# Down weights of a ConvFFN: loads apart from their parts and begun within the up stage, sums on VectorE, another order of products, the last pair loaded twice

## The chip, the cores and the metric

The kernel runs on one core of one Trainium2 chip. The metric is the device time of one launch in microseconds, the median of several runs. One execution was also recorded by the hardware profiler; all rows below are from that one. In rows, PE is TensorE's matmuls, PEld its weight loads, DVE is VectorE, ACT ScalarE, POOL GpSimd and SP (SPq for its DMA issues) SyncE. "L1226" is line 1226 of the kernel before.

## The reference

One step of a hybrid network over 2048 latent tokens (on a grid 64 wide) and 128 context tokens, width 1024: an HGRN2 mixer, then a ConvFFN, then a final norm. The part that matters here is the ConvFFN, with 2816 inner channels:

```
def conv_ffn(h, w_up, conv_w, conv_b, w_down, grid_axis):
    a, g = jnp.split(h @ w_up, 2, axis=-1)
    a = token_conv(a, conv_w, conv_b, grid_axis)
    return (jax.nn.silu(a) * g) @ w_down
```

`token_conv` adds, for each channel, the neighbours left and right with weights of their own. The result is added to the stream under a gate, and `rms_norm` follows.

## The kernel before

Every float32 product is made of three float16 products: an operand is split into a high part (ScalarE, `A.activation` with `Copy`) and the rest (VectorE), and high x high, high x low and low x high are summed in PSUM. In rows such parts of the down weights are `wd`: L1226 makes the high part on ScalarE, L1227 the low part on VectorE, both from `rawd`, the float32 block loaded from memory.

Both matrix products of the ConvFFN over latent tokens use a Strassen-Winograd scheme: blocks of 2 x 2, seven products instead of eight. `PROD` names for each product the weight block or sum (A11 to A22, S1 to S4), the token block or sum (B11, T1, ...) and the PSUM bank (A, B or C) that it accumulates in. The context tokens use the plain three products (`mm3`).

The **up stage** goes over pairs of channel blocks (`cb` = 0, 2, ... 20) and in each over four pieces `p` of 512 latent tokens; after p = 1 the context follows (`up_ctx`). A pass `up(cb, p)` has seven products for two column blocks, 14 x 12 matmuls of 256 columns. Between products, `post()` runs one step of each of the generators that wait in `gates` and `pending`: `gate` does the convolution (L1103 on ScalarE, L1110 and L1112 on VectorE), silu (L1137), the multiplication by g (L1139), and the sums and splits of the tokens that the down stage needs (L1147 to L1151, L970, L971), and stores them in memory (`ud`, `uc` for the context). `c` are the products' results in SBUF: L1085 to L1097 put them there from PSUM on ScalarE, L1082 adds to them on VectorE.

The **down stage** holds all weights in SBUF: four pairs `i` of output blocks, for each four blocks A11 to A22 (`blocks_down`) and four sums S1 to S4 (`sums_down`), each 128 x 1408. The token side is read from memory again (`load_ut`, tiles `U`), one product ahead. First come the context (`down_ctx`) and product 1 of the first piece, pair by pair, then all other products of the four pieces in the order of `todo`; each adds its result to `x` at once (L1303, for the context L1270), and after the last that touches a half the final norm runs (`final_norm`, L360 to L368).

Each engine works through its own list in order. The lists are written by a scheduler that may move an instruction of the program ahead of others on the same engine, and the places of SBUF tiles are found by `place()` from the tiles' lifetimes in program order: a tile waits until the last reader of what lay there before is done. All loads and stores go through SyncE's one queue.

Of the kernel before, what the change touches and what calls it, by code (L numbers as in the profile page):

```python
# [23 lines left out]
NCTX = 128  # L24
NTOK = NLAT + NCTX
NCB = 22
# [82 lines left out]
def place(tiles, far):  # L109
# [6 lines left out]
    for grain, lo, hi, some in (  # L116
# [5 lines left out]
        some.sort(key=lambda i: (age(i) < NEVER // 2, size(i) != 11, age(i) <= AGE,  # L122
                                 -min(size(i), 16), tiles[i].born))
        tight = []
        while True:
            lives = [[] for _ in range(slots)]
            bad = None
            for i in some:
# [5 lines left out]
                if n == 11:  # L134
                    cap = 1
# [79 lines left out]
def stages(nc, tl, pt, drt, xT, adaH, adaT, pvec, w_in, w_out, w_up, w_down, state, yT, st_out):  # L215
# [944 lines left out]
    def up(cb, p):  # L1160
# [5 lines left out]
        for i in (1, 2, 6, 5, 7, 3, 4):  # L1166
            while any(PROD[i][0] not in WQ.get((cb, j), {}) for j in range(2)):
                post()
            for j in range(2):
                product(qs[j], i, WQ[cb, j], TT[p])  # L1170
            post()
            tick()
        gates.append(gate(cb, p, *qs))
# [55 lines left out]
    def blocks_down(i):  # L1229
        load_rd(i)  # L1230
# [4 lines left out]
        a11, a12, a21, a22 = (RD[i][z] for z in ("A11", "A12", "A21", "A22"))  # L1235
        G.tensor_tensor(a22, a21, a22, ALU.add)
        G.tensor_tensor(a21, a11, a21, ALU.subtract)
        G.tensor_tensor(a11, a22, a11, ALU.subtract)
        G.tensor_tensor(a12, a12, a11, ALU.subtract)

    def sums_down(i):
        for z, b in (("S2", "A11"), ("S1", "A22"), ("S3", "A21"), ("S4", "A12")):
            part(i, z, RD[i][b])
            yield

# [123 lines left out]
    for cb in range(0, NCB, 2):  # L1369
        last = cb + 2 == NCB  # L1370
        for p in range(CTX):
# [5 lines left out]
            if last and p < 2:  # L1377
                pending.append(blocks_down(p))
            if last and p == 2:
                while pending:  # L1380
                    post()
                load_uc()
                for j in range(2):
                    load_xd(CTX, j, 0, NCTX)
    while gates:
        post()
    load_ut(0, PROD[1][1])
    load_xd(0, 0, 0)
    pending.extend([blocks_down(2), blocks_down(3), *(sums_down(i) for i in range(MP))])
    for i in range(MP):  # L1390
        while "A22" not in DW[i]:
            post()
        down_ctx(i)
        tick()
        post()
        if i % 2:
            down(0, 1, (i - 1, i))
    final_norm(CTX, 0, NCTX)
    NEED = {1: (0, 0), 6: (0, 1), 5: (1, 1), 4: (1, 0)}
    todo = [(p, n) for p in range(CTX)  # L1400
            for n in ((1, 2, 6, 5, 7, 3, 4), (1, 6, 5, 7, 3, 2, 4))[p == CTX - 1]]
    for k, (p, n) in enumerate(todo):
        if k + 1 < len(todo):
# [4 lines left out]
        if k + 1 < len(todo) and n1 in NEED:  # L1408
# [5 lines left out]

# [46 lines left out]
```

## Time and profile before

| what | value |
| --- | --- |
| median of three runs | 2813.37 us (2812.61 to 2813.89) |
| profiled execution | 2808.24 us |
| span in its profile | 2806.1 us |
| mean granted clock of TensorE | 0.990 |
| busy TensorE / VectorE / ScalarE / GpSimd | 2707.9 / 1896.1 / 1068.8 / 131.8 us |

The profiled execution's time is its span and some 2 us around it. Busy times are sums over an engine's instructions; matmuls that run at the half clock count with their longer time. The up stage lies between about 1395 and 2307 us, the down stage behind it.

### The profile page before, as it was taken

To read this page: it belongs to the slowest core of one execution; us is meant where nothing else is said; L and a number is where in the kernel's file an instruction comes from. 1 tells how busy PE (TensorE), PEld (TensorE's weight loads), DVE (VectorE), ACT (ScalarE), POOL (GpSimd) and SP (SyncE) were. 2 spreads that over 40 slices of the span, in tenths; PEclk is the share of its full clock that TensorE was granted. 3 is DMA by queue.
4 is the path that set the end of the run, shared out by engine and by line. 5 is a ranking of instruction groups with operands and counts; after the bars stand their busy time and mean duration, and the time that the engine had idled before them with its cause. 6 is when DMAs were issued, how large, how long until landed. Compare 5 with 4: busy or idle time off the path is not lost.

```text
span 2806.1 us, 57255 instructions
## 1 busy us (share of the span) xinstructions
PE 2707.9 (97%) x23576; PEld 2129.9 (76%) x23576; DVE 1896.1 (68%) x5308; ACT 1068.8 (38%) x2373; POOL 131.8 (5%) x100
## 2 busy tenths in 40 slices
PE   8999999999999999999999999999999976999998
PEld 4677777777777776754588888888888866888887
DVE  7987788878876677746996767676666777233133
ACT  5533333333334342424664545454445433000001
POOL 0100000000000000000000000000000124000000
PEclk9999999999999999999999999999999998999999
DMA  7021212121101010434122222222221353343342
GB/s 269 20 63 40 78 34 77 43 70 45 66 9 51 9 52 16 148 111 179 61 59 82 60 77 80 70 73 74 84 86 57 101 170 110 106 153 133 125 147 88
DMA packets 188309, 236.85 MB, mean 84 GB/s; under 512 B 12304, under 2 KB 142736, under 8 KB 188048
## 3 DMA queue, kind: packets, MB, share of 16 engines
q1 hardware_dynamic: 188048, 233.19, 26.3%
q8 instruction: 185, 3.03, 0.4%
q14 instruction: 76, 0.62, 0.1%
HBM read 163.55 MB, written 69.60 MB: 83 GB/s over the span
## 4 chain that ended last, share of the span: by engine, by line
PE 72%; DVE 15%; DMA 5%; ACT 3%; issue 2%; POOL 0%; SPq 0%; DVEq 0%; POOLq 0%; ACTq 0%
PE pj_p L1076 11%; PE pj_p L1294 10%; PE sc_p L1076 8%; PE pj_p L417 7%; PE pj_p L418 7%; PE pj_p L416 7%; PE pj_p L540 4%; PE pj_p L538 4%; PE pj_p L539 4%; PE sc_p L692 2%; PE sc_p L1294 2%; DMA ud<-u 2%; DMA r<-w_up 1%; PE sc_p L652 1%; PE sc_p L661 1%
## 5 line engine op out<-in xcount | busy, mean ns | idle before, releaser
L1076 PEld LDWEIGHTS <-w 128*128 128x128 f16 x7392 | 725.3, 98 | 126.0 <-issue 40.0
L1076 PE MATMUL pj_p<-T,w 128*128 128x256 f16 x4224 | 491.4, 274 | 33.8 <-DVE c L1082 10.4
L1294 PEld LDWEIGHTS <-wd 128*128 128x128 f16 x3696 | 364.7, 99 | 80.7 <-issue 19.7
L1294 PE MATMUL pj_p<-U,wd 128*128 128x256 f16 x3168 | 358.5, 274 | 21.4 <-DVE x L1303 11.7
L1076 PE MATMUL sc_p<-T,w 128*128 128x256 f16 x3168 | 369.2, 273 | 1.6 <-ACT c L1091 1.6
L416 PE MATMUL pj_p<-H,wp 128*128 128x512 f16 x768 | 290.6, 379 | 3.7 <-ACT H L395 3.4
L417 PE MATMUL pj_p<-H,wp 128*128 128x512 f16 x768 | 291.7, 380 | 0.9 <-DVE H L400 0.9
L418 PE MATMUL pj_p<-H,wp 128*128 128x512 f16 x768 | 291.6, 380 | 0.0
L540 PE MATMUL pj_p<-wp,H 128*128 128x256 f16 x1024 | 279.2, 273 | 0.0
L539 PE MATMUL pj_p<-wp,H 128*128 128x256 f16 x1024 | 279.1, 273 | 0.0
L538 PE MATMUL pj_p<-wp,H 128*128 128x256 f16 x1024 | 279.1, 273 | 0.0
L1303 DVE SCALAR_TENSOR_TENSOR x<-pj_p,g,x 128x256 f32<-128x256 f32 x96 | 46.3, 483 | 231.9 <-PE pj_p L1294 227.5
L418 PEld LDWEIGHTS <-wp 128*128 128x128 f16 x960 | 94.0, 98 | 91.4 <-issue 2.2
L416 PEld LDWEIGHTS <-wp 128*128 128x128 f16 x960 | 94.2, 98 | 83.9 <-issue 4.4
L417 PEld LDWEIGHTS <-wp 128*128 128x128 f16 x960 | 94.0, 98 | 80.8 <-issue 1.4
L1103 ACT ACTIVATE y<-c,pv,cws 128x512 f32<-128x512 f32 x88 | 71.4, 813 | 153.2 <-DVE c L1082 147.1
L363 ACT ACTIVATE n<-x 128x256 f32<-128x256 f32 (+1 forms) x63 | 23.4, 398 | 277.2 <-DVE x L1303 225.2
L511 ACT ACTIVATE f<-pj_p 128x512 f32<-128x512 f32 x64 | 38.1, 597 | 196.4 <-PE pj_p L418 196.4
L540 PEld LDWEIGHTS <-H 128*128 128x128 f16 x1024 | 100.2, 98 | 11.9
L539 PEld LDWEIGHTS <-H 128*128 128x128 f16 x1024 | 100.2, 98 | 11.8
L538 PEld LDWEIGHTS <-H 128*128 128x128 f16 x1024 | 100.3, 98 | 11.5
L417 PE MATMUL pj_p<-og,wo 128*128 128x512 f16 (+1 forms) x320 | 108.7, 349 | 0.0
(281 smaller groups left out, 5095.3 us busy)
## 6 DMA issues: line engine op xcount, KB each, us to landing
ud<-u SPq DMA_DIRECT2D x44, 896.0 KB, 4.8
U<-ud SPq DMA_DIRECT2D x56, 704.0 KB, 4.5
r<-w_up SPq DMA_DIRECT2D x44, 512.0 KB, 3.7
wr<-w_in SPq DMA_DIRECT2D x40, 512.0 KB, 4.2
wr<-adaT SPq DMA_DIRECT2D x32, 512.0 KB, 3.6
rawd<-w_down SPq DMA_DIRECT2D x16, 704.0 KB, 6.3
x<-xT SPq DMA_DIRECT2D x32, 256.0 KB, 5.4
sp<-oT SPq DMA_DIRECT2D x32, 256.0 KB, 2.5
```

The source lines that it names most:

```text
L416: T.matmul(out, whl[0], hhl[:, 0, :n], start=first, stop=False)
L417: T.matmul(out, whl[0], hhl[:, 1, :n], start=False, stop=False)
L418: T.matmul(out, whl[1], hhl[:, 0, :n], start=False, stop=last)
L511: A.activation(ft, pj[:, :n], AF.Tanh, scale=0.5 * IWS)
L538: T.matmul(o, hp[k][:, 0, tok], wvg[0][:, k], start=(k == 0), stop=False)
L539: T.matmul(o, hp[k][:, 0, tok], wvg[1][:, k], start=False, stop=False)
L540: T.matmul(o, hp[k][:, 1, tok], wvg[0][:, k], start=False, stop=(k == KT - 1))
L692: T.matmul(pkv[:, d, cc_], un["kT"][:, d, cc_], vt[:, cc_], start=True, stop=True)
L1076: T.matmul(out, wt[:, a, ks], tt[:, b, k], start=first and k == 0 and n == 0, stop=i in (2, 3, 4) and k == 3 and n == 2, skip_group_check= ...
L1103: A.activation(y, a, AF.Identity, bias=pv[:, PV_CB + cb : PV_CB + cb + 1], scale=cws[:, 22 + cb : 23 + cb])
L1294: T.matmul(out, w[:, a, k], UT[p, zb][b][:, k], start=first and i % 2 == 0 and k == 0 and q == 0, stop=n in (2, 3, 4) and k == KP - 1 and ...
L1303: V.scalar_tensor_tensor(x, get(src), g64[:, 1, m, 0:1], x, ALU.mult, ALU.add)
```

## The change

What it does: the raw loads of the down weights (`load_rd`) stand apart from the making of their parts, and the loads for pairs 0 to 2 are issued while the last pair of channel blocks is still in the up stage. There too, behind product 6 of the last pass, the context's tokens (`load_uc`), the first `U` and the `x` of context and first piece are loaded. The sums S1 to S4 are made by VectorE instead of GpSimd, and the parts S2 and S3 are made for each pair right behind its sums, S1 and S4 of all pairs afterwards. Product 1 of the first two pairs comes before the context of pair 2, and the context of pair 3 behind product 1 of all pairs. The four raw blocks of pair 3 are loaded a second time for the sums. All four pieces use the order 1, 2, 6, 7, 4, 5, 3, and `place()` treats tiles of 22 grains as those of 11 (a grain is 512 bytes of a partition; `rawd`, `wd` and `U` have 11).

```
--- before.py
+++ after.py
@@ -119,7 +119,7 @@
         slots = (hi - lo) // grain
         size = lambda i: -(-tiles[i].size // grain)
         age = lambda i: tiles[i].last - tiles[i].born
-        some.sort(key=lambda i: (age(i) < NEVER // 2, size(i) != 11, age(i) <= AGE,
+        some.sort(key=lambda i: (age(i) < NEVER // 2, size(i) not in (11, 22), size(i) != 11, age(i) <= AGE,
                                  -min(size(i), 16), tiles[i].born))
         tight = []
         while True:
@@ -131,7 +131,7 @@
                 for a, b in tight:
                     if t.born <= b and a <= t.last:
                         cap >>= 1
-                if n == 11:
+                if n in (11, 22):
                     cap = 1
                 cap = max(cap, 1)
                 room = []
@@ -1170,6 +1170,12 @@
                 product(qs[j], i, WQ[cb, j], TT[p])
             post()
             tick()
+            if i == 6 and cb + 2 == NCB and p + 1 == CTX:
+                load_uc()
+                load_ut(0, "B11")
+                for j in range(2):
+                    load_xd(CTX, j, 0, NCTX)
+                load_xd(0, 0, 0)
         gates.append(gate(cb, p, *qs))
 
     def gate_ctx(cb, a, g):
@@ -1227,21 +1233,28 @@
         V.scalar_tensor_tensor(t[:, 1], src, WS, t[:, 0], ALU.mult, ALU.subtract)
 
     def blocks_down(i):
-        load_rd(i)
         for z in ("A11", "A12", "A21", "A22"):
             part(i, z, RD[i][z])
             yield
 
-        a11, a12, a21, a22 = (RD[i][z] for z in ("A11", "A12", "A21", "A22"))
-        G.tensor_tensor(a22, a21, a22, ALU.add)
-        G.tensor_tensor(a21, a11, a21, ALU.subtract)
-        G.tensor_tensor(a11, a22, a11, ALU.subtract)
-        G.tensor_tensor(a12, a12, a11, ALU.subtract)
-
-    def sums_down(i):
-        for z, b in (("S2", "A11"), ("S1", "A22"), ("S3", "A21"), ("S4", "A12")):
-            part(i, z, RD[i][b])
+    def sums_down(pairs):
+
+        for i in pairs:
+            a11, a12, a21, a22 = (RD[i][z] for z in ("A11", "A12", "A21", "A22"))
+            V.tensor_tensor(a22, a21, a22, ALU.add)
+            V.tensor_tensor(a21, a11, a21, ALU.subtract)
             yield
+            V.tensor_tensor(a11, a22, a11, ALU.subtract)
+            V.tensor_tensor(a12, a12, a11, ALU.subtract)
+            yield
+            part(i, "S2", a11)
+            yield
+            part(i, "S3", a21)
+            yield
+        for i in pairs:
+            for z, b in (("S1", "A22"), ("S4", "A12")):
+                part(i, z, RD[i][b])
+                yield
 
     def load_xd(p, j, h, n=HN):
 
@@ -1374,44 +1387,46 @@
                 up_ctx(cb)
                 if not last:
                     pending.extend([quad(cb + 2, 0), quad(cb + 2, 1)])
-            if last and p < 2:
-                pending.append(blocks_down(p))
-            if last and p == 2:
-                while pending:
-                    post()
-                load_uc()
-                for j in range(2):
-                    load_xd(CTX, j, 0, NCTX)
-    while gates:
-        post()
-    load_ut(0, PROD[1][1])
-    load_xd(0, 0, 0)
-    pending.extend([blocks_down(2), blocks_down(3), *(sums_down(i) for i in range(MP))])
-    for i in range(MP):
-        while "A22" not in DW[i]:
-            post()
+            if last and p == 0:
+                load_rd(0)
+            if last and p == 1:
+                load_rd(1)
+                load_rd(2)
+                pending.extend([blocks_down(0), blocks_down(1)])
+    load_rd(3)
+    load_ut(0, "B21")
+    for i in range(2):
         down_ctx(i)
         tick()
         post()
-        if i % 2:
-            down(0, 1, (i - 1, i))
+    pending.append(blocks_down(2))
+    down(0, 1, (0, 1))
+    while "A22" not in DW[2]:
+        post()
+    down_ctx(2)
+    pending.append(blocks_down(3))
+    down(0, 1, (2, 3))
+    while "A22" not in DW[3]:
+        post()
+    down_ctx(3)
     final_norm(CTX, 0, NCTX)
-    NEED = {1: (0, 0), 6: (0, 1), 5: (1, 1), 4: (1, 0)}
-    todo = [(p, n) for p in range(CTX)
-            for n in ((1, 2, 6, 5, 7, 3, 4), (1, 6, 5, 7, 3, 2, 4))[p == CTX - 1]]
+    load_rd(3)
+    pending.append(sums_down(range(MP)))
+    tick()
+    NEED = {1: (0, 0), 6: (0, 1), 7: (1, 1), 4: (1, 0)}
+    todo = [(p, n) for p in range(CTX) for n in (1, 2, 6, 7, 4, 5, 3)]
     for k, (p, n) in enumerate(todo):
-        if k + 1 < len(todo):
+        if k + 1 < len(todo) and k:
             p1, n1 = todo[k + 1]
             load_ut(p1, PROD[n1][1])
         if k:
             down(p, n)
-        if k + 1 < len(todo) and n1 in NEED:
+        if k and k + 1 < len(todo) and n1 in NEED:
             load_xd(p1, *NEED[n1])
         if n in (3, 4):
             final_norm(p, int(n == 3), HN)
     while norms:
         tick()
-
 
 # ---- launch: one core; inputs laid out by the host, outputs as the reference has them ----
```

The lists of instructions, as the scheduler orders them. GpSimd's list in the down stage, difference of the two kernels, its first sums (`rawd` are the raw blocks, the sums overwrite them):

```order
-L1236 TENSOR_TENSOR rawd_28490<-rawd_28488,rawd_28490 128x1408
-L1237 TENSOR_TENSOR rawd_28488<-rawd_28484,rawd_28488 128x1408
-L1238 TENSOR_TENSOR rawd_28484<-rawd_28490,rawd_28484 128x1408
-L1239 TENSOR_TENSOR rawd_28486<-rawd_28486,rawd_28484 128x1408
-L1236 TENSOR_TENSOR rawd_28928<-rawd_28926,rawd_28928 128x1408
```

All 16 are gone from this list. VectorE's list around the start of the down stage, from the last gate's multiplication (L1139) to the first read of product 1's result into `x`, before (`wd` is a low part, `y` the gate's tile; conv and context rows left out):

```order
L1139 TENSOR_TENSOR y_29286<-y_29286,c_2960_29072 128x1024
...
L1227 SCALAR_TENSOR_TENSOR wd_29659<-rawd_29651,wd_29659 128x1408
...
L1227 SCALAR_TENSOR_TENSOR wd_29606<-rawd_29460,wd_29606 128x1408
L1227 SCALAR_TENSOR_TENSOR wd_29464<-rawd_29456,wd_29464 128x1408
L1227 SCALAR_TENSOR_TENSOR wd_29848<-rawd_28490,wd_29848 128x1408
...
L1227 SCALAR_TENSOR_TENSOR wd_29662<-rawd_29653,wd_29662 128x1408
...
L1227 SCALAR_TENSOR_TENSOR wd_29609<-rawd_29462,wd_29609 128x1408
L1303 SCALAR_TENSOR_TENSOR x_29315<-pj_p_29612,g_2050_15449,x_29315 128x256
```

and now:

```order
L1139 TENSOR_TENSOR y_29443<-y_29443,c_2960_29058 128x1024
...
L1233 SCALAR_TENSOR_TENSOR wd_29666<-rawd_28810,wd_29666 128x1408
...
L1233 SCALAR_TENSOR_TENSOR wd_29851<-rawd_29295,wd_29851 128x1408
L1233 SCALAR_TENSOR_TENSOR wd_29622<-rawd_28804,wd_29622 128x1408
L1233 SCALAR_TENSOR_TENSOR wd_29854<-rawd_29297,wd_29854 128x1408
...
L1244 TENSOR_TENSOR rawd_28810<-rawd_28808,rawd_28810 128x1408
L1233 SCALAR_TENSOR_TENSOR wd_29896<-rawd_29301,wd_29896 128x1408
...
L1245 TENSOR_TENSOR rawd_28808<-rawd_28804,rawd_28808 128x1408
L1233 SCALAR_TENSOR_TENSOR wd_29625<-rawd_28806,wd_29625 128x1408
L1247 TENSOR_TENSOR rawd_28804<-rawd_28810,rawd_28804 128x1408
L1316 SCALAR_TENSOR_TENSOR x_29167<-pj_p_29586,g_2050_15449,x_29167 128x256
```

Between the same two rows stand now two more kinds of row, the sums L1244, L1245 and L1247, among the parts (now L1233); parts for the pairs 2 and 3 are mixed. SyncE's list in the last block of the up stage, before (`ud` and `uc` are stores of u, the others are loads):

```order
L1251 DMA x_29061<-xsp_17507 128x128 x4
L1222 DMA rawd_28488<-w_down 128x11x128
L1222 DMA rawd_28490<-w_down 128x11x128
L1158 DMA ud_15452<-u_28622 1792x1x256
L1222 DMA rawd_28924<-w_down 128x11x128
L1185 DMA uc<-u_28811 128x256
L1222 DMA rawd_28926<-w_down 128x11x128
L1185 DMA uc<-u_28881 128x256
L1222 DMA rawd_28922<-w_down 128x11x128
L1222 DMA rawd_28928<-w_down 128x11x128
L1158 DMA ud_15453<-u_28908 1792x1x256
```

and now:

```order
L1228 DMA rawd_28800<-w_down 128x11x128
L1158 DMA ud_15452<-u_28606 1792x1x256
L1228 DMA rawd_28804<-w_down 128x11x128
L1228 DMA rawd_28806<-w_down 128x11x128
L1228 DMA rawd_28798<-w_down 128x11x128
L1228 DMA rawd_28796<-w_down 128x11x128
L1228 DMA rawd_28808<-w_down 128x11x128
L1228 DMA rawd_28810<-w_down 128x11x128
L1191 DMA uc<-u_28795 128x256
L1158 DMA ud_15453<-u_28908 1792x1x256
L1191 DMA uc<-u_28881 128x256
L1270 DMA U_29149<-uc 128x2816
```

Raw loads that stood one or two at a time between the stores now stand ahead of them, and those of `U` follow right behind the stores.

## Rows read from the trace of the kernel before

**Rows 1.** The page, its part on busy time: busy us of each engine, share of the span and number of instructions.

```profile
PE 2707.9 (97%) x23576; PEld 2129.9 (76%) x23576; DVE 1896.1 (68%) x5308; ACT 1068.8 (38%) x2373; POOL 131.8 (5%) x100
```

**Rows 2.** Busy time by stretches around the end of the up stage: stretch, its length, then for PE, PEld, DVE, ACT and POOL busy us and instructions, last PE's granted clock, the DMA share and GB/s.

```profile
2204.00:2250.00 46.00, 42.99 (x435) 38.38 (x434) 34.34 (x41) 20.09 (x36) 12.45 (x4) 1.00 0.40 110
2250.00:2300.00 50.00, 33.55 (x273) 28.25 (x273) 38.84 (x48) 21.05 (x42) 14.31 (x5) 0.88 0.52 154
...
2350.00:2400.00 50.00, 28.59 (x190) 21.73 (x189) 29.10 (x25) 14.17 (x17) 12.72 (x4) 0.76 0.19 60
```

**Rows 3.** The waits of TensorE between 2204 and 2430 us, longest sums first: line, what it waited for, us in total, times, longest.

```profile
PE pj_p L1076 <- ACT c L1089: 8.8, 1, 8.8
PE pj_p L1294 <- DVE x L1303: 8.5, 4, 4.9
PE sc_p L1294 <- DMA U<-ud: 7.3, 1, 7.3
PE pj_p L1076 <- ACT y L1199: 5.4, 1, 5.4
PE pj_p L1294 <- DMA U<-ud: 4.8, 2, 3.9
PE pj_p L1294 <- ACT wd L1226: 3.7, 1, 3.7
```

**Rows 4.** Groups of TensorE's instructions between 2204 and 2430 us, by form: line, names, shapes, count, busy us and mean ns of one, idle time before them. L1294 are the down products, L1076 the up products; L416 is the first of the three lines of `mm3`, each with the same count.

```profile
L1294 PE MATMUL pj_p<-U,wd 128*128 128x256 f16 x400 | 49.7, 288 | 18.2 <-DVE x L1303 8.5 <-DMA U<-ud 4.8 <-ACT wd L1226 3.7
L1076 PE MATMUL pj_p<-T,w 128*128 128x256 f16 x387 | 47.7, 282 | 18.0 <-ACT c L1089 8.8 <-ACT y L1199 5.4 <-ACT y L1198 2.3
L1076 PE MATMUL sc_p<-T,w 128*128 128x256 f16 x288 | 34.8, 279 | 1.4 <-ACT c L1091 1.4
...
L416 PE MATMUL pj_p<-U,wd 128*128 128x128 f16 x176 | 29.6, 219 | 0.0
...
L1294 PE MATMUL sc_p<-U,wd 128*128 128x256 f16 x132 | 17.9, 303 | 7.7 <-DMA U<-ud 7.3 <-DVE x L1303 0.5
L416 PE MATMUL pj_p<-T,w 128*128 128x128 f16 x32 | 5.4, 219 | 0.0
```

**Rows 5.** The course of TensorE: start, us, instruction, count in a row, idle time before it and who ended it. The first row is the first matmul of the down stage; the second and third are the first and last of 77 matmuls of 128 columns that lie in between, one row each.

```profile
2307.51 0.22 PE L416 MATMUL pj_p<-U,wd 128*128 128x128 f16 x1
...
2339.80 0.22 PE L416 MATMUL pj_p<-U,wd 128*128 128x128 f16 x1
...
2344.04 0.22 PE L417 MATMUL pj_p<-U,wd 128*128 128x128 f16 x1
...
2387.46 6.63 PE L1294 MATMUL sc_p<-U,wd 128*128 128x256 f16 x33 [7.29 <-DMA U<-ud]
...
2403.70 3.77 PE L1294 MATMUL sc_p<-U,wd 128*128 128x256 f16 x33
2407.30 5.51 PE L1294 MATMUL pj_p<-U,wd 128*128 128x256 f16 x49
```

**Rows 6.** The course of GpSimd between 2230 and 2370 us: the first and the last of its 16 sums, which are all that it does there.

```profile
2237.32 3.22 POOL L1236 TENSOR_TENSOR rawd<-rawd,rawd 128x1408 f32<-128x1408 f32 x1 [832.95 <-PE pj_p L1076]
...
2357.91 4.42 POOL L1239 TENSOR_TENSOR rawd<-rawd,rawd 128x1408 f32<-128x1408 f32 x1
```

**Rows 7.** The course of VectorE: two rows from beside GpSimd's first sums, and one from between them and the next four, when GpSimd does nothing.

```profile
2237.55 3.27 DVE L1151 TENSOR_TENSOR t<-y,t 128x256 f32<-128x256 f32 x1
2240.74 0.74 DVE L1082 SCALAR_TENSOR_TENSOR c<-pj_p,c 128x256 f32<-128x256 f32 x2
...
2267.17 0.41 DVE L1151 TENSOR_TENSOR t<-y,t 128x256 f32<-128x256 f32 x1
```

**Rows 8.** The chain that ended last, two pieces of it: start, us on the chain, what.

```profile
2280.09 6.64 DVE y L1110 x2
...
2290.21 3.63 DVE y L1112
...
2298.22 1.87 PE pj_p L1076 x8
...
2381.49 5.93 DMA U<-ud
```

**Rows 9.** Groups of VectorE's instructions between 2204 and 2430 us, by form, columns as in rows 4.

```profile
L1227 DVE SCALAR_TENSOR_TENSOR wd<-rawd,wd 128x1408 f16<-128x1408 f32 x32 | 66.9, 2103 | 29.0 <-ACT wd L1226 29.0
...
L1139 DVE TENSOR_TENSOR y<-y,c 128x1024 f32<-128x1024 f32 x5 | 6.1, 1225 | 4.7 <-ACT y L1137 4.7
```

**Rows 10.** The course of VectorE behind the end of the up stage, with GpSimd idle: the last conv from its first to its last row, and two low parts in a row.

```profile
2308.46 1.39 DVE L1110 SCALAR_TENSOR_TENSOR y<-c,cws,y 128x504 f32<-128x504 f32 x2
...
2315.22 0.42 DVE L1151 TENSOR_TENSOR t<-y,t 128x256 f32<-128x256 f32 x1
...
2322.08 3.16 DVE L1227 SCALAR_TENSOR_TENSOR wd<-rawd,wd 128x1408 f16<-128x1408 f32 x2 [0.30 <-ACT wd L1226]
```

**Rows 11.** The course of ScalarE: two high parts of down weights that wait for their raw blocks.

```profile
2274.04 1.38 ACT L1226 ACTIVATE wd<-rawd 128x1408 f16<-128x1408 f32 x1 [2.13 <-DMA rawd<-w_down]
2276.30 1.38 ACT L1226 ACTIVATE wd<-rawd 128x1408 f16<-128x1408 f32 x1 [0.88 <-DMA rawd<-w_down]
```

**Rows 12.** The waits of TensorE in the whole execution, columns as in rows 3: up products for VectorE's adds, and norms.

```profile
PE pj_p L1076 <- DVE c L1082: 10.4, 12, 2.5
...
PE sc_p L368 <- DVE n L364: 5.2, 6, 1.6
```

## Prediction, made before the changed kernel ran

> **What bounds the kernel now.** I read the page first, then the busy time by stretches, the waits of TensorE, and last the engines beside it. The page's first line [rows 1] has TensorE busy in 97% of the span, so time can only come from the 3% or from matmuls that run slowly while they count as busy. The table by stretches [rows 2] shows where both lie: between 2250 and 2300 us TensorE is busy 33.55 of 50 us at a granted clock of 0.88, between 2350 and 2400 us 28.59 of 50 at 0.76. That is the passage from the up stage to the down stage, which is what the change rewrites.
>
> How much is lost there: between 2204 and 2430 us (226 us) TensorE runs 400 + 387 + 288 + 132 = 1207 matmuls of 256 columns, and 3 x (176 + 32) = 624 of 128 columns [rows 4]. Undisturbed, 33 of the first kind go by in 3.60 us (2403.70 to 2407.30), 0.109 each, and 77 of the second kind in 4.24 us, 0.055 each [rows 5]. So the work is 1207 x 0.109 + 624 x 0.0556 = 131.8 + 34.7 = 166.5 us, and **59.5 us are lost**. The waits of that window say to whom: six rows add up to 38.5 us [rows 3]. The other 21 us are smaller waits and half clock: after one wait 33 matmuls take 6.63 us, later 3.77 [rows 5]. Some 24.6 us of the loss fall before the up stage ends at 2307.51 [rows 5], since 672 + 96 matmuls, 73.4 + 5.3 us, fill the 103.3 us from 2204.2 on.
>
> The waits have one root more than their names tell. GpSimd runs 16 sums of the down weights, the first at 2237 us in 3.2 us, the last at 2358 in 4.4 [rows 6]. Beside one of them VectorE's L1151 takes 3.27 us; without one the same operation takes 0.41. L1082, which reads one operand from PSUM, stays short beside them (two in 0.74) [rows 7]. The chain that ended last shows the price [rows 8]: two conv operations L1110 take 6.64 us, L1112 another 3.63 in the chain, the gate comes late, and TensorE's next matmul stands at 2298.22, after the longest wait of the window, 8.8 us. In the second half the weights' low parts (L1227) and the loads are late: the load of U that TensorE waits for 7.3 us is issued only at 2381.49 and takes 5.93 [rows 8].
>
> The Trainium skill (SBUF — State Buffer, Who interferes with whom) says that a VectorE operation with two SBUF inputs and a GpSimd operation that reads SBUF exclude each other for a whole instruction; the split between L1151 and L1082 agrees.
>
> **The change part by part.**
> Sums moved. The 16 sums leave GpSimd, and VectorE is rid of the stretching: the 32 parts L1227 take 66.9 us in the window [rows 9] where two in a row take 3.16 undisturbed [rows 10], 1.54 each, or 49. VectorE gets the sums instead. No row shows one of that size there; a TENSOR_TENSOR of 1024 columns takes 1.23 [rows 9], a part of 1408 columns 1.54, and on GpSimd it was 3.2: I take 1.54, nearest in size and also with two SBUF inputs, bounds 1.23 and 3.2. 16 x 1.54 = 24.6 us (20 to 51), which replace at least 17 us of stretched parts and the stretched conv operations. By the rule above, what the two engines share falls by 16 x (3.2 - 1.54) = 27 us; taken as the whole gain, that gives 2808.2 - 27 + 5.1 = 2786. Rival 2 is that case, worked out from the rows.
>
> Loads. The raw blocks are asked for during the last up block: in the order of SyncE's queue eleven raw loads, with one store of u between them, stand ahead of the next two stores of `uc`; before, each store stood behind one or two. What they cost: two queued raw blocks land 2.26 us apart (ScalarE's parts start at 2274.04 and 2276.30, each released by its load) [rows 11]. About eight of them are still to be moved when the stores come, which makes 18 us. In p = 2 of the last block ScalarE's parts need places which those stores free, and ScalarE's evictions for TensorE stand behind the parts: by counting along the queues I get a wait of 3 to 5 us there and 0.4 in p = 3. Bounds: 0.4 if the loads drain faster, 10 if they drain as slowly as the 5.93 us load. I take 4.5. For the loads of U, `uc` and x of the down stage the earlier issue takes the 7.3 and 4.8 us rows [rows 3] away: they are asked for during p = 3 and a product ahead. SyncE's queue itself is held by the store of the last u, but the next U load still comes a product early.
>
> Order at the start of the down stage. After the up stage TensorE has two context pairs (2 x 2 x 66 matmuls of 128 columns, 14.7 us) and product 1 of the first pairs (3.6 us) before it needs pair 2: 18.3 us after the end E of the up stage. In VectorE's order, from the last conv to the low part of A12 of pair 2, stand the conv chain (2308.46 to 2315.64 today [rows 10], some 5.4 us without the L971 and the hand-over to ScalarE in it), 7 parts and 4 sums (11 x 1.54 = 17 us) and some 2 us of small reads. It begins 1.4 us before E, and with a microsecond of hand-overs ends near E + 24: a **wait of 5 to 6 us**, bounds 3 and 10, and 2 us of half clock behind it. After that the parts S2 and S3 come in pairs ahead of their products. Two norms and two late x reads of the context add 3 us, by the 0.9 us that such waits take (six in 5.2 us) [rows 12].
>
> Second load of pair 3: four loads on SyncE, asked for around the context's last pair, some 15 us ahead of the sum that reads them; four queued take 4 x 2.3 = 9 us. Hidden by product 1 of the last pairs and context pair 3; 2 to 5 us if that cover goes.
>
> Other order of products, number of matmuls and tail: the same matmuls, and behind the last product the same norm. Nothing. `place()` has no tile of 22 grains here, but new lifetimes give new places, and with them another order on VectorE, ScalarE and SyncE from the first mixer on. TensorE's waits for VectorE's L1082 are 12 today, 10.4 us [rows 12]; a few more of 1 to 2 us are likely, a few less possible. I take 3 us, bounds -5 and +15.
>
> **Sum.** Losses left in the passage: 4.5 + 0.4 + 5.5 + 2 + 3 = 15.4, say 16 (bounds 6 and 29). Gain 59.5 - 16 - 3 = 40.5. The profiled execution took 2808.2 us (span 2806.1, and 2.1 around it) and comes to 2767.7; the median of the runs before is 5.1 above their profiled execution, so the **forecast is 2773 us**.
>
> **The rivals.**
> 1. The forecast: 11 to 28 us of losses left in all (19 in the sum): 2765 to 2782. Chance 0.55.
> 2. VectorE becomes the bound of the passage. For it: 48 sums and parts of 1.54 us are 74 us, more than the stretched 66.9 of the parts today, and they come in bunches. Against it: today VectorE is busy 38.84 of 50 us in the worst stretch [rows 2], and the stretching of L1227 alone is 17 us of its busy time in the passage. If all the sums beyond the four already counted lie on TensorE's path, 12 x 1.54 = 18.5 more are lost: 2791. Chance 0.17.
> 3. Nearly all of it vanishes: waits of 6 us remain and the new order costs nothing: 2808.2 - 53.5 + 5.1 = 2760. Chance 0.12.
> 4. The row of loads blocks. All eleven loads land before the stores, ScalarE stands behind its parts, and p = 2 and p = 3 each wait the 10 us of the upper bound: 15 us more, 2788. The Trainium skill (DMA: Bandwidth & Descriptors, Two DMAs through the same engine are not ordered) has descriptors of one queue start in order, which is this mechanism; no row of before shows so many in a row. Chance 0.08.
> 5. Slower than before. The new places chain VectorE's late adds (L1082) to TensorE in every up block: it needs more than 40 us, 3.7 us in each of the 11 blocks, where today the longest such wait is 2.5 [rows 12]; at 4.5 us each the time is 2822. Chance 0.04.
> 6. No change that can be measured: the sums of VectorE delay as much as those of GpSimd did, 2813. Chance 0.04.
>
> **How the numbers follow.** 0.2% is 5.6 us, about what a measurement can tell from no change. Rivals 1 to 4 are faster by more: 0.92; 0.04 the same, 0.04 slower. The range leaves out the lower half of 3 and the worst of 2, and all of 5 and 6: 2760 to 2793.
>
> **What would show it.** In the profile after, no sum on GpSimd, L1151 and L1110 at 0.4 and 0.7 us throughout, TensorE busy over 90% in every 50 us from 2200 on, and the up stage's end near 2288 (2307.51 - 24.6 + 4.9). A wait for the low part of pair 2's A12 or for the x read beside it of 5 to 6 us is the largest left. The sums on VectorE take 1.54 each. Wrong would be: sums of 3 us, TensorE waiting for ScalarE in p = 2 for 10 us, waits on the S parts, or an up stage that already ends later than before at its start.

## The result, and the profile after

| | before | after |
| --- | --- | --- |
| median on the chip of the comparison | 2812.99 us (4 runs) | 2775.01 us (4 runs, 2773.41 to 2777.14) |
| ratio, 95% interval | | 0.9865 [0.9848, 0.9882] |
| profiled execution, its span | 2808.24, 2806.1 us | 2777.14, 2775.2 us |
| again, on a second chip | 2808.18 us | 2776.31 us, ratio 0.9884 [0.9868, 0.9901] |

The forecast was 2773 us, in a range from 2760 to 2793. The two profiled executions lie 31 us apart and the medians 38 on one chip and 32 on the other: the profiled execution of before lies 5 us under the median of its kernel, that of after 2 us above. What follows compares traces with traces.

The stretches of [rows 2] in the profile after, and the one between them, with the same columns (busy us and instructions of PE, PEld, DVE, ACT and POOL, then PE's granted clock, DMA share, GB/s):

```profile
2204.00:2250.00 46.00, 46.00 (x423) 41.24 (x422) 32.03 (x59) 24.09 (x49) 0.00 (x0) 1.00 0.44 120
2250.00:2300.00 50.00, 47.05 (x463) 41.71 (x461) 39.41 (x58) 26.44 (x48) 0.00 (x0) 0.97 0.76 221
2300.00:2350.00 50.00, 44.54 (x612) 42.12 (x610) 35.64 (x48) 17.14 (x23) 0.00 (x0) 0.93 0.50 145
2350.00:2400.00 50.00, 45.24 (x446) 40.14 (x444) 37.26 (x44) 20.82 (x19) 0.55 (x1) 1.00 0.55 172
```

The stretches with TensorE busy for only 33.55 and 28.59 us of 50 are gone, and GpSimd's column is empty but for one instruction of 0.55 us. VectorE is busy 2.3 us less than before in the first stretch, 0.6 more in the second and 8.2 more in the last. The waits of TensorE in the passage, which answer to [rows 3]:

```profile
PE pj_p L418 <- DVE wd L1233: 3.7, 1, 3.7
PE pj_p L1076 <- ACT c L1089: 2.9, 1, 2.9
PE pj_p L1307 <- DVE x L1316: 2.8, 3, 1.3
PE pj_p L416 <- ACT wd L1232: 1.6, 1, 1.6
PE sc_p L368 <- DVE n L364: 1.1, 1, 1.1
PE sc_p L1307 <- DVE x L1316: 1.0, 1, 1.0
```

These are all of them and add up to 13.1 us, where the six longest of before had 38.5. VectorE's groups in the same stretch, for [rows 7, 9]:

```profile
L1233 DVE SCALAR_TENSOR_TENSOR wd<-rawd,wd 128x1408 f16<-128x1408 f32 x31 | 49.7, 1621 | 16.2 <-ACT wd L1232 16.2
...
L1110 DVE SCALAR_TENSOR_TENSOR y<-c,cws,y 128x504 f32<-128x504 f32 x10 | 7.3, 740 | 9.5 <-ACT y L1103 9.5
...
L1244 DVE TENSOR_TENSOR rawd<-rawd,rawd 128x1408 f32<-128x1408 f32 x4 | 6.5, 1617 | 0.0
...
L1151 DVE TENSOR_TENSOR t<-y,t 128x256 f32<-128x256 f32 x5 | 2.1, 417 | 0.0
```

A part takes 1.62 us where its mean was 2.10, L1151 takes 0.42 in each of the five, and a sum on VectorE 1.62.

For all that follows the span is cut at three points, found by counting TensorE's matmuls in each trace: the first up product (the up stage begins), the first product of the last up block, and the end of the fourth product of the first piece. Between the second and the third lies the **passage**; the matmuls in each part are the same in number in all kernels.

| kernel | up stage begins | last block begins | passage | rest | span |
| --- | --- | --- | --- | --- | --- |
| before | 1391.3 | 2204.2 | 225.7 | 376.3 | 2806.1 |
| after | 1396.1 | 2219.0 | 184.8 | 371.4 | 2775.2 |
| after again | 1395.7 | 2218.4 | 184.5 | 371.4 | 2774.4 |
| e1 after, sums on GpSimd | 1396.2 | 2215.6 | 209.8 | 371.6 | 2797.0 |
| e2 before, sums on VectorE | 1389.2 | 2203.8 | 210.6 | 375.3 | 2789.8 |
| e3 before, order of products | 1389.7 | 2204.7 | 233.5 | 375.6 | 2813.8 |
| e4 before, places of after | 1396.9 | 2214.9 | 234.7 | 375.0 | 2824.5 |
| e5 after, quads' loads together | 1384.3 | 2190.5 | 192.9 | 373.8 | 2757.2 |
| e6 after, late tokens | 1394.8 | 2218.4 | 203.7 | 373.5 | 2795.6 |
| e7 after, late raw loads | 1382.7 | 2199.7 | 197.2 | 372.0 | 2768.9 |
| e8 after, no second load | 1397.0 | 2213.0 | 200.6 | 377.0 | 2790.6 |
| e9 as e5, norm later | 1429.1 | 2235.0 | 182.5 | 377.3 | 2794.8 |
| e10 as e9, places of e5 | 1384.9 | 2192.0 | 193.0 | 373.7 | 2758.7 |

So the change gave 40.9 us in the passage and 4.9 behind it, and took 14.9 ahead of it, in stages whose code it doesn't touch. The experiments ask three things: what gave the 40.9, what cost the 14.9, and whether the second can be had back.

One thing belongs beside the table: which of the kernels have their tiles at the same places. `place()` counts the operations of all engines alike, so e1 has every tile where after has it, and e2 every tile where before has it. e3 keeps the first 3025 of the 3180 places of before, and e6 all but 94 of the first 2961 of after. In e5, e7, e8 and e9 some nine tenths of the tiles lie elsewhere than in the kernel that was edited. Places alone move the passage too: e4, which differs from before in nothing else, took 9.0 us more there, and e9 and e10, which differ only in places, lie 10.5 us apart. So the 12 and 16 us found for e7 and e8 below may be partly that.

### The profile page after: what moved, and what is told of

Its sections match the earlier page's. It is cut to its first block, busy times and chain, and to the rows that moved or that the text cites. A ratio compares the mean times of both kernels' runs of the same rounds, so it can differ in the third digit from the quotient of the medians.

```text
span 2775.2 us, 57195 instructions
## 1 busy us (share of the span) xinstructions
PE 2705.4 (97%) x23576; PEld 2129.1 (77%) x23576; DVE 1886.0 (68%) x5324; ACT 1071.8 (39%) x2373; POOL 72.9 (3%) x84
## 4 chain that ended last, share of the span: by engine, by line
PE 58%; DVE 16%; DMA 5%; ACT 2%; issue 2%; POOL 0%; SPq 0%; DVEq 0%; POOLq 0%; ACTq 0%
PE pj_p L1307 11%; PE pj_p L1076 9%; PE sc_p L1076 6%; PE pj_p L418 5%; PE pj_p L416 5%; PE pj_p L417 5%; DMA r<-w_up 3%; PE pj_p L539 3%; PE pj_p L538 3%; PE pj_p L540 3%; DMA ud<-u 2%; DVE u L971 2%; PE sc_p L1307 1%; PE sc_p L692 1%; DVE wd L1233 1%
## 5 line engine op out<-in xcount | busy, mean ns | idle before, releaser
L1076 PEld LDWEIGHTS <-w 128*128 128x128 f16 x7392 | 725.0, 98 | 115.4 <-issue 29.7
L1076 PE MATMUL pj_p<-T,w 128*128 128x256 f16 x4224 | 491.0, 274 | 24.2 <-DVE c L1082 16.4
L1076 PE MATMUL sc_p<-T,w 128*128 128x256 f16 x3168 | 367.8, 273 | 0.0
L416 PE MATMUL pj_p<-H,wp 128*128 128x512 f16 x768 | 291.2, 380 | 2.8 <-ACT H L395 2.4
L1316 DVE SCALAR_TENSOR_TENSOR x<-pj_p,g,x 128x256 f32<-128x256 f32 x96 | 46.4, 483 | 211.6 <-PE pj_p L1307 211.5
L416 PEld LDWEIGHTS <-wp 128*128 128x128 f16 x960 | 94.3, 98 | 83.5 <-issue 4.2
L539 PEld LDWEIGHTS <-H 128*128 128x128 f16 x1024 | 100.2, 98 | 11.8
```

Of the source, the lines that this page charges most:

```text
L416: T.matmul(out, whl[0], hhl[:, 0, :n], start=first, stop=False)
L539: T.matmul(o, hp[k][:, 0, tok], wvg[1][:, k], start=False, stop=False)
L1076: T.matmul(out, wt[:, a, ks], tt[:, b, k], start=first and k == 0 and n == 0, stop=i in (2, 3, 4) and k == 3 and n == 2, skip_group_check= ...
L1316: V.scalar_tensor_tensor(x, get(src), g64[:, 1, m, 0:1], x, ALU.mult, ALU.add)
```

## Experiments

### The sums, alone and taken away (e2, e1)

e2 is the kernel before with one letter changed in four lines:

```
-        G.tensor_tensor(a22, a21, a22, ALU.add)
+        V.tensor_tensor(a22, a21, a22, ALU.add)
...
```

> The kernel before, with its 16 sums made by VectorE; nothing else changed. Theory: the waits of 8.8, 5.4 and 2.3 us in the last up block and their half clock go, some 20 us, while the U load that is issued late and the waits on parts stay: 2790 us (2782 to 2798). Rival: VectorE, with 24.6 us more to do and the loads as late as before, becomes what TensorE waits for: 2805 to 2818 us.

Measured: 2791.5 us beside 2807.8, ratio 0.9945 [0.9929, 0.9962]; the passage takes 210.6 us, 15.1 less than before. Its waits:

```profile
PE pj_p L1294 <- DVE x L1303: 11.2, 3, 10.3
PE sc_p L1294 <- DMA U<-ud: 6.8, 1, 6.8
...
PE pj_p L1076 <- ACT c L1089: 1.8, 2, 1.3
```

The wait of 8.8 us behind the stretched conv has shrunk to 1.3, as the theory has it; with all places kept, the 15.1 us are the sums' alone. What stays is the late load of U, as in [rows 3], and a longer wait for an x read behind VectorE's fuller list.

e1 is the reverse, the kernel after with `G.tensor_tensor` in the four lines of `sums_down`.

> The kernel after, with its 16 sums of the down weights made by GpSimd again; all else as after. Theory (GpSimd's sums stretch VectorE's operations with two SBUF operands, and through them the gates and the parts): L1110, L1112 and L1151 beside a sum take 3 us again, TensorE waits in p = 2 and p = 3 of the last block and for the parts, 2795 us (2788 to 2808). Rival (the earlier loads and the order do it, the engine of the sums hardly matters): 2772 to 2780 us, with VectorE relieved of 24.6 us of sums.

Measured: 2798.7 us beside 2807.8, ratio 0.9968 [0.9958, 0.9978]; the passage takes 209.8 us, 25.0 more than after, again with all places kept.

```profile
PE sc_p L1307 <- DVE x L1316: 12.4, 1, 12.4
PE pj_p L1076 <- ACT c L1089: 7.1, 2, 4.8
...
L1233 DVE SCALAR_TENSOR_TENSOR wd<-rawd,wd 128x1408 f16<-128x1408 f32 x32 | 62.2, 1965 | 24.5 <-ACT wd L1232 24.5
L1110 DVE SCALAR_TENSOR_TENSOR y<-c,cws,y 128x504 f32<-128x504 f32 x10 | 8.9, 896 | 10.1 <-ACT y L1103 10.1
```

The parts are stretched again, 1.97 us in the mean for 1.62, although VectorE has 16 operations fewer to do. Single conv operations take 2.3 and 3.5 us for 0.74, and one L1147 and one L1148 3.1 and 3.4 for 0.42; L1151, which the expectation named, stood beside no sum and kept its 0.42. The four passages together: 225.7 with neither, 210.6 with the sums alone, 209.8 with all but the sums, 184.8 with both. Each half gives 15 to 16 us and both give 41, so the same sums are worth 15.1 us in the kernel before and 25.0 beside the other edits. The waits suggest why: while the late loads still hold TensorE, part of what the sums free goes into the next wait (the x read of 10.3 us in e2). That is a reading of the waits. And "all but the sums" holds the loads, the order and new places, which these four kernels don't separate.

### The loads (e7, e6, e8)

e7 puts the raw loads back to their parts; the parts of pair 0 may then also begin one pass earlier, and the rest is as after:

```
+        load_rd(i)
         for z in ("A11", "A12", "A21", "A22"):
...
-            if last and p == 0:
-                load_rd(0)
...
+            if last and p < 2:
+                pending.append(blocks_down(p))
```

> The kernel after; the raw loads of each pair of the down weights are issued by the generator that makes its parts, as in the kernel before, the rest as after. Theory: the parts of pairs 0 to 3 wait for their loads one after the other and come some 10 us late, the passage takes 195 to 205 us, with TensorE's waits on wd and x of 10 us and more. Rival (the loads can hardly start earlier for want of places, and the row of loads delays p = 2): 180 to 187, and the wait of 2.9 us in p = 2 is gone.

Measured: 2770.6 us (one run) and a passage of 197.2 us, 12.4 more than after, with these waits:

```profile
PE pj_p L416 <- ACT wd L1232: 9.1, 1, 9.1
PE sc_p L368 <- DVE n L364: 5.5, 1, 5.5
```

The size lies in the theory's range and the first wait is its mechanism: the part that TensorE waits 9.1 us for had waited for its raw block, as nine others of ScalarE's did, by 0.6 to 7.2 us; in after none did. The wait at the norm is less clearly so, since e5 below, with early loads, has 4.1 us there. The whole is faster than after all the same, since its early stages are 19 us shorter (table), 13 of them in the mixer, whose code is the same.

e6 issues the loads of `uc`, the first U and x behind the up stage instead of behind product 6 of its last pass.

> The kernel after; the loads of uc, the first U and the x of context and first piece are issued behind the up stage instead of within its last pass. The passage (from the first matmul of the last up block to the end of product 7 of the first piece) takes 184.8 us in the trace of after and 225.7 in that of before. Theory: TensorE waits for uc at the start of the down stage, some 6 us and half clock behind it: 190 to 196 us. Rival (the store of the last u holds SyncE's queue anyway, or the wait for pair 2's part absorbs it): 183 to 187.

Measured: 2797.3 us (one run), a passage of 203.7 us, 18.9 more than after. The expectation had 5 to 11.

```profile
PE pj_p L416 <- DMA U<-uc: 13.6, 1, 13.6
```

One of the two halves of `uc` is not only issued later: it now stands in SyncE's list behind all four raw loads of pair 3 and the store of u among them, so that 13.6 us are waited where 6 were expected. A wait of 4.6 us at the norm, 1.1 in after, is the next longest. As most places are kept, this is the cleanest of the three experiments on loads.

e8 leaves out the second `load_rd(3)`, so that the sums of pair 3 use the first load's blocks.

> The kernel after without the second load of pair 3: its sums use the raw blocks of the first load, which are kept until then. Theory (the second load is hidden, and costs and gives nothing): the passage takes 184 to 187 us. Rival (it takes bandwidth that others need, or frees places that the kept blocks now deny to the U loads): below 182, or above 190.

Measured: 2792.4 us (one run), a passage of 200.6 us, 15.8 more than after. TensorE waits 13.4 us for the norm of the context at L368. VectorE's course ahead of it:

```profile
2352.14 0.34 DVE L1283 SCALAR_TENSOR_TENSOR x<-pj_p,g,x 128x128 f32<-128x128 f32 x1
2352.40 0.28 DVE L364 TENSOR_TENSOR n<-n,n 128x128 f32<-128x128 f32 x1
2352.59 1.62 DVE L1233 SCALAR_TENSOR_TENSOR wd<-rawd,wd 128x1408 f16<-128x1408 f32 x1
2354.13 0.28 DVE L364 TENSOR_TENSOR n<-n,n 128x128 f32<-128x128 f32 x1
2354.33 1.62 DVE L1248 TENSOR_TENSOR rawd<-rawd,rawd 128x1408 f32<-128x1408 f32 x1
2355.87 0.28 DVE L364 TENSOR_TENSOR n<-n,n 128x128 f32<-128x128 f32 x1
```

Seven adds of 0.28 us each stand one by one between sums and parts of 1.6 us, and some of the parts wait for ScalarE. In after, one part and no sum stands among the seven adds, and TensorE's wait there is 1.1 us. So the wait of 13.4 us comes from the order of VectorE's list. That the second load as such sets this order is not shown: without it, nine tenths of the tiles lie elsewhere too, and this run doesn't tell the two apart.

### The order of products (e3)

The kernel before with the new order for all four pieces, and x loaded for product 7 instead of 5:

```
-            for n in ((1, 2, 6, 5, 7, 3, 4), (1, 6, 5, 7, 3, 2, 4))[p == CTX - 1]]
+            for n in (1, 2, 6, 7, 4, 5, 3)]
```

> The kernel before, with the order of products of the kernel after in the four pieces (1, 2, 6, 7, 4, 5, 3, and x loaded for product 7 instead of 5). Theory from the two traces, where each of the last three pieces is some 1.6 us shorter in the kernel after: 5 us faster, 2808 us, and no wait of TensorE for the norm's L364 within the pieces. Rival (the pieces gain from something else of the change): 2813 us within 1.

Measured: 2814.1 us beside 2807.8, ratio 1.0018 [1.0008, 1.0028], so slower by a little; the expectation missed. The passage is 7.8 us longer: product 7 needs S3, which the kernel before makes third of each pair's sums, and the waits for x reads there are 13.5 us instead of 8.5.

```profile
PE pj_p L1294 <- DVE x L1303: 13.5, 3, 5.7
```

So the new order alone doesn't pay; whether it does together with the new order of parts, no run tests by itself. And behind the passage it gives 0.7 us, not 5. In the kernel after and in e1 that part is 4.7 to 4.9 us shorter than before, and TensorE has no wait at the norm (L368) within the pieces; here each of the first three pieces has two such waits, of 0.2 to 0.7 us. The order of products is not what decides it: e8 and e9 have the same order, and both the waits and 377.0 and 377.3 us behind the passage. e9 and e10 differ only in their places, and e10 takes 373.7, so places move this part as well. What made it 371.4 in the kernel after stays open.

### The places (e4, e5, after again, e9, e10)

The kernel before, with 2918 of its 3180 tiles at the places which `place()` gives them in the kernel after (a table, PLACES), the rest placed around them:

```
+                if i < len(PLACES):
+                    at[i], t, s = PLACES[i], tiles[i], (PLACES[i] - lo) // grain
+                    for lv in lives[s : s + size(i)]:
+                        bisect.insort(lv, (t.born, t.last))
```

> The kernel before, with each SBUF tile born before the last block's down loads (2918 of 3180) at the place that it has in the kernel after; the rest is placed around them. The order of VectorE's list is then that of the kernel after for its first 4560 instructions, up to the last block. Theory (the places alone make the early stages slower): the last block begins some 10 to 15 us later than in the trace before, and the whole takes 2823 us (2818 to 2830). Rival (the later begin in the one trace is chance of that execution): 2810 to 2816 us.

Measured: 2823.8 us, ratio 1.0055 [1.0042, 1.0069], and the last block begins at 2214.9 us, 10.7 later than before. So most of the early loss is the places'. They also cost 9.0 us in the passage, which takes 234.7 us here, although the code is that of before. The second profile of the kernel after has the last block at 2218.4 us, 0.6 from the first: it is no chance of one execution either.

> The kernel after, a second time, beside the kernel before on the same chip: a ratio of 0.986 to 0.988. Theory (its early loss lies in the order of its lists and comes back in each execution): the last up block begins at 2216 to 2221 us (2219.0 in the first trace, 2204.2 in the kernel before), the passage takes 183 to 188 us (184.8). Rival (the early loss was chance of one execution): the last block begins before 2211 us.

Where it comes from is to be read in the trace of after. VectorE's course in block 5, with the time that it stood idle and the releaser in brackets:

```profile
1781.22 2.49 DVE L1038 SCALAR_TENSOR_TENSOR w<-s,w 128x512 f16<-128x512 f32 x4
1788.76 0.69 DVE L1048 TENSOR_TENSOR s<-r 128x512 f32<-128x512 f32 x1 [5.04 <-DMA r<-w_up]
1789.37 0.42 DVE L1082 SCALAR_TENSOR_TENSOR c<-pj_p,c 128x256 f32<-128x256 f32 x1
```

L1048 is the first sum of the second weight quad of the next block. Its two raw loads are issued at 1779.47 and 1781.33 us, each just behind a part of the first quad (L1038), because their tiles have that quad's places; VectorE stands 5 us, and the add L1082 that TensorE waits for is behind it. e5 issues the loads of both quads together, for all blocks but the last, so that they cannot share places:

```
-                    pending.extend([quad(cb + 2, 0), quad(cb + 2, 1)])
+                    quads = [quad(cb + 2, 0), quad(cb + 2, 1)]
+                    if cb + 4 < NCB:
+                        for q in quads:
+                            next(q)
+                    pending.extend(quads)
```

> The kernel after; the raw loads of the second up quad of a block (L1043, for all blocks but the last) are issued together with those of the first, so that their tiles no longer take the first quad's places. Theory (in the trace of after, VectorE stands in blocks 5 to 9 at L1048, the first sum of the second quad, whose raw load can start only when the first quad's parts are made, and the adds L1082 behind it hold TensorE some 2 us in each block): those waits go, the last block begins near 2207 us instead of 2219, and the whole takes 2764 us (2759 to 2770). Rival (the new places cost elsewhere as much, or the load is late for another reason): 2772 to 2780 us.

Measured: **2759.65 us** beside 2807.2, ratio 0.9831 [0.9815, 0.9848], faster than both kernels. TensorE's waits for L1082 from the start of the up stage to the last block, in after and in e5:

```profile
PE pj_p L1076 <- DVE c L1082: 16.4, 14, 2.6
```

```profile
PE pj_p L1076 <- DVE c L1082: 2.9, 3, 1.5
```

The theory's wait is gone, but the gain ahead of the last block is 28.5 us, more than twice the 13.5 that this wait explains: 11.8 of it lie in the mixer, where nothing was changed but the places. Nor is it shown that the shared places were the cause of the wait, since e5 also issues the second quad's loads earlier. VectorE's L1048 from the start of the up stage to the last block, in after, e8 and e5:

```profile
L1048 DVE TENSOR_TENSOR s<-r 128x512 f32<-128x512 f32 x20 | 13.8, 690 | 37.5 <-DMA r<-w_up 33.1 <-issue 4.3
```

```profile
L1048 DVE TENSOR_TENSOR s<-r 128x512 f32<-128x512 f32 x20 | 13.7, 687 | 39.9 <-DMA r<-w_up 39.9
```

```profile
L1048 DVE TENSOR_TENSOR s<-r 128x512 f32<-128x512 f32 x20 | 13.7, 687 | 9.4 <-DMA ud<-u 6.5 <-DMA r<-w_up 2.6
```

In e8 the two quads' tiles lie apart from the third block to the tenth, and VectorE stands as long as in after; SyncE's loads of L1043 wait there for readers of other tiles (97.3 us in all for L1112). So keeping the two quads apart is not enough by itself. And the passage grew from 184.8 to 192.9 us:

```profile
PE pj_p L418 <- DVE wd L1233: 5.6, 2, 3.6
PE sc_p L368 <- DVE n L364: 4.1, 1, 4.1
```

e9 takes e5 and begins the context's final norm behind product 2 of the first piece instead of ahead of the second load.

> The kernel of the experiment with both up quads' loads together (2759.7 us), and the context's final norm begun behind product 2 of the first piece instead of ahead of the reload. In its trace TensorE waits 4.1 us at the norm's matmul L368 for VectorE's last L364 and runs at half clock behind it. Theory: with products in between the wait and its half clock go, the passage of 192.9 us falls to 184 to 188, the whole takes 2754 us (2749 to 2758). Rival (VectorE's list is reordered, and the adds of the norm or the parts S2 and S3 hold TensorE at the next x read as long): 2757 to 2766 us.

Measured: 2795.5 us, beyond both the theory and the rival. The passage fell to 182.5 us, better than the theory, and the up stage began at 1429.1 us, 44.9 later than in e5: one line moved at the end of the program, and the mixer at its start became slower. To separate the two, e10 is e9 with the places of e5 in a table (six small tiles of the norm moved).

> The kernel of the norm begun later, but with every SBUF tile at the place that it has in the kernel with both quads' loads together (six small tiles of the norm, which would overlap, moved), written into the kernel as a table instead of found by place(). VectorE's order is then that of the latter for its first 4716 instructions, up to the context's last pair. Theory (where the norm begins is worth some 8 us in the passage, and the 45 us by which the mixer's end differed between those two kernels came from the places alone): the up stage begins at 1382 to 1387 us (1384.3 there, 1429.1 with the norm later), the passage takes 183 to 188 us (192.9 and 182.5), the whole 2751 us (2747 to 2756). Rival (the norm's place in the program moved the early stages by itself): the up stage begins after 1400 us.

Measured: 2760.5 us beside 2811.9, ratio 0.9824 [0.9811, 0.9837], the same as e5. The up stage begins at 1384.9 us, so the 45 us were the places alone. But the passage takes 193.0 us, where 183 to 188 were expected: beginning the norm later is worth nothing. Its wait went to the next x read, in this kernel (its lines are 55 lower down) the second of these rows:

```profile
PE pj_p L473 <- DVE wd L1288: 4.8, 2, 3.6
PE sc_p L1362 <- DVE x L1371: 3.9, 1, 3.9
```

The good passage of e9 belonged to its places as well: there TensorE waits 0.3 + 0.3 us on the parts of pair 2.

## Why the prediction was right

The time, 2775 for 2773, is closer than the terms. Against the two traces: forecast were 43.5 us of gain in the passage (59.5 - 16), nothing behind it, and 3 lost ahead of it; found were 40.9, 4.9 and 14.9. The sum, 40.5, was 30.9 between the traces. That the time came out within 2 us is partly luck, as the end of this section shows.

**The sums on VectorE: right.** 1.54 us was taken, and three parts in a row take 4.68 us, a single sum 1.62. VectorE's work did not hold TensorE for more than the term that I had for it, so rival 2 fell; e1 shows that a VectorE with fewer operations but stretched ones is the slower.

**The row of loads in p = 2: right in place and mechanism.** Forecast 3 to 5 us, taken at 4.5, found 2.9 (L1089 in the waits above). ScalarE's course:

```profile
2267.80 0.38 ACT L1089 ACTIVATE c<-pj_p 128x256 f32<-128x256 f32 x1 [0.61 <-PE pj_p L1076]
2274.22 1.38 ACT L1232 ACTIVATE wd<-rawd 128x1408 f16<-128x1408 f32 x1 [6.04 <-DMA uc<-u]
2275.50 0.37 ACT L1089 ACTIVATE c<-pj_p 128x256 f32<-128x256 f32 x1
```

A part waits 6 us for the store of `uc`, whose place it needs, and the eviction L1089 stands behind it. Rival 4 was the same with 10 us and more; it did not come to that. The up stage's last block with the context takes 83.8 us; forecast were the same (2288 - 2204.2).

**The wait for pair 2: right.** Forecast 5 to 6 us near 24 us after the up stage's end. It ends at 2302.8, and TensorE's course has 1.59 + 3.70 = 5.3 us, the second ending 24.1 us behind:

```profile
2322.91 0.23 PE L416 MATMUL pj_p<-U,wd 128*128 128x128 f16 x1 [1.59 <-ACT wd L1232]
2322.97 0.22 PE L417 MATMUL pj_p<-U,wd 128*128 128x128 f16 x1
2326.89 0.29 PE L418 MATMUL pj_p<-U,wd 128*128 128x128 f16 x1 [3.70 <-DVE wd L1233]
```

VectorE has been busy without a gap from 2311 us on, with sums among the parts as its list has them:

```profile
2315.49 4.68 DVE L1233 SCALAR_TENSOR_TENSOR wd<-rawd,wd 128x1408 f16<-128x1408 f32 x3
2320.09 0.34 DVE L1283 SCALAR_TENSOR_TENSOR x<-pj_p,g,x 128x128 f32<-128x128 f32 x1
2320.35 1.62 DVE L1244 TENSOR_TENSOR rawd<-rawd,rawd 128x1408 f32<-128x1408 f32 x1
2321.88 1.62 DVE L1233 SCALAR_TENSOR_TENSOR wd<-rawd,wd 128x1408 f16<-128x1408 f32 x1
...
2323.68 1.62 DVE L1245 TENSOR_TENSOR rawd<-rawd,rawd 128x1408 f32<-128x1408 f32 x1
2325.21 1.62 DVE L1233 SCALAR_TENSOR_TENSOR wd<-rawd,wd 128x1408 f16<-128x1408 f32 x1
```

**Norms and late x reads: mis-sized.** Forecast 3 us, found 1.1 + 2.8 + 1.0 = 4.9, and the late x reads were those of the first piece (L1316), not of the context. All waits together came to 13.1 us, and 13.4 had been forecast. The passage lost 18 us instead of 16 because the remainder, half clock and small gaps, was some 5 us and had been put at 2; the granted clock between 2310 and 2330 us was 0.84.

**The second load: not confirmed, without effect on the sum.** It was priced as hidden work that gives nothing. In e8 taking it away cost 15.8 us, with another order of VectorE's list and other places; which of the load and the places did it is open.

**Other order of products: nothing, was wrong by 4.9 us.** The pieces became shorter. In e3 the order alone gives 0.7 of it, and e8 and e9 have the order without the gain.

**The places: mis-sized, the largest error.** 3 us were taken, with a bound of 15, and 14.9 found. The term was guessed from the rows of one kind of wait (12 of L1082, 10.4 us in [rows 12]); these became 14 with 16.4 us, and 4.9 us more were lost in the mixer, which I had not looked at. e4 has 10.7 us of it with nothing but the places. The 4 us between it and the kernel after are not explained; e1, with every place of after, begins the last block at 2215.6 us, so about as much can come about at unchanged places.

**The signs named in advance.** GpSimd's sums are gone and the sums take 1.6 us, as said. But the up stage ends at 2302.8 us and not near 2288, one stretch of 50 us has TensorE busy for 44.54, just under 90%, and the up stage was late from its start, which stood among the signs of being wrong.

The errors of 12 us ahead of the passage and 5 behind it partly cancelled. With 3 us in the passage they left the gain between the traces 10 us too large. Some 7 of these were covered by chance: the median of before lay 5 us above its profiled execution, as the sum assumed for after too, but that of after lay 2 below its own. On the second chip the medians lie 31.9 us apart, where 40.5 were forecast. The mechanisms in the passage were foreseen; the time within 2 us was not earned by the terms.

## What to carry to other kernels

The same edit can be worth more beside another (the sums 15 us in the one kernel and 25 in the other, at unchanged places), so a change that seems small alone is to be tried with its partner before it is thrown away. Where a planner places tiles or a scheduler orders lists, every edit is two edits: compare the stages that the code didn't touch, and fix the old places in a table before judging the edit itself, as e10 did. When an engine waits, look at what stands in front of the late instruction in its list, not only at who is busy: seven adds of 0.28 us among operations of 1.6 us held TensorE for 13.4 us in e8.

## What the runs showed that I had not expected

The mixer, which no kernel here changes, ended between 1382.7 and 1429.1 us with different places of its tiles. Two executions of the same program differ by 0.4 us (1396.1 and 1395.7), and the kernels with the same places in the mixer by 2.1 (1389.2 to 1391.3 in before, e2 and e3, 1394.8 to 1396.9 in after, e1, e4 and e6). And the granted clock after the passage's waits stayed mild: 0.93 in the worst stretch of 50 us after, where [rows 2] had 0.76.
